# Joining the value and score products of a dilated attention pipeline at the end of an item's 4th and 8th step, with two small moves beside it

## The chip, the cores and the metric

One NeuronCore of a Trainium2 chip runs the whole kernel. Five engines work side by side, each on its own queue of instructions in a fixed order: TensorE (PE, matmuls; its weight loads are shown as PEld), VectorE (DVE), ScalarE (ACT), GpSimd (POOL) and SyncE (SP, which here issues the DMA transfers). They wait for each other by semaphores. SBUF is the working memory of 128 partitions, PSUM the eight banks into which TensorE writes.

The metric is the device time of one execution in microseconds. Before the change it is 1513.78 us, the median of three runs (1512.96 to 1514.76).

## The reference

An encoder block over 1024 positions of 1024 channels, batch 1, in float32. One input projection feeds three mixers; each is gated, projected back, merged with sigmoid gates and passed through an output projection. The part that the change touches is the dilated sliding-window attention: 24 heads of 64 channels, in three groups of eight with the windows and dilations (128, 1), (512, 4) and (2048, 16), whose outputs are merged by the softmax of their log-denominators.

```python
A_GROUPS = ((128, 1), (512, 4), (2048, 16))
...
def dilated_window_attention(q, k, v, window, dilation):
    half = window // (2 * dilation)
    ...
    sc = jnp.einsum('znqhd,znkhd->znhqk', qb, kw).astype(jnp.float32) * (dh ** -0.5)
    sc = jnp.where(valid[None, :, None], sc, NEG_INF)
    m = jnp.max(sc, axis=-1, keepdims=True)
    p = jnp.exp(sc - m)
    l = jnp.sum(p, axis=-1, keepdims=True)
    o = jnp.einsum('znhqk,znkhd->znqhd', (p / l).astype(v.dtype), vw)
    lse = (m + jnp.log(l))[..., 0]
    ...
def reference(x, mem, ...):
    h = rms_norm(x, g_pre[layer])
    a_qkv, bq, bk, bv, mq, ga, gb, gm, mg = jnp.split(h @ w_in[layer], split_at, axis=-1)
    aq = rope(a_qkv[:, :, 0], pos)
    ak = rope(a_qkv[:, :, 1], pos)
    ...
    wts = jax.nn.softmax(jnp.stack(lses, axis=0), axis=0).astype(dt)
    oa = jnp.einsum('gbsh,gbshd->bshd', wts, jnp.stack(outs, axis=0)).reshape(b, s, BRANCH_WIDTH)
    # two more mixers: ob (full attention), om (attention into a memory)
    ya = (oa * jax.nn.silu(ga)) @ w_br_a[layer]
    ...
    merged = gates[:, :, 0] * ya + gates[:, :, 1] * yb + gates[:, :, 2] * ym
    x = x + rms_norm(merged @ w_out[layer], g_post[layer])
```

## The kernel before

Every projection is made of *units* (`add_unit`, L195): 128 output channels over 1024 positions, in two halves of 512. A half is 24 matmuls of `dense` (L139): for each of eight slices of the channels three products (L143, L145, L147) of a rounded high part and a rest of both operands, all into one of two PSUM banks `d`. A unit's weights come by a DMA into one of two buffers `wr` (L114), ScalarE rounds them into `wh` (L105) and VectorE takes the rest into `wl` (L106); this is done one unit ahead.

TensorE's order is written out by hand. `weave` (L174) takes dense matmuls one by one from a generator and puts pieces of attention between them so that both come to their end together: after each piece as many dense matmuls follow as its estimated cost is worth. The order in the other engines' queues is left to a scheduler that follows the program's order and its own estimates.

The dilated attention has twelve *items* (`seq`, L1128): four pairs of heads by three groups. While item n is in work, the three dense units of item n + 1 run: queries, keys, values, 48 matmuls each. Queries and keys are evacuated by `rope_half` (L821): per half, VectorE multiplies the bank by sine and cosine into `t2a` and `t1a` (four products of 32 partitions and one of 128, L830 or L831), and GpSimd adds the two into `aq` or `ak` (L837). For groups 1 and 2 that sum reorders positions into residue classes, so that each half of the positions is spread over the whole tile. The values are evacuated into `vta` (L862).

An item has eight tiles T of 128 queries and these pieces (L1022 to L1030):

- `scores(b)`, for four tiles at a time, into four PSUM banks (L918);
- `soft(T)`: VectorE applies the mask and takes the minimum (L930), ScalarE the exponentials with their sums (L933 to L938), into one of five `pra` buffers;
- `trans(T)`: TensorE transposes the probabilities into the one bank `tr` (L955, L964), ScalarE copies them to `app` (L967);
- `values(i0)`: the values are transposed through the same bank (L895) and copied by ScalarE (L897);
- `pv(b)`: value products for four tiles (L981), copied by ScalarE to `og` (L989);
- `stats`: minima and sums are transposed through the bank `tr` (L1000), copied by VectorE into `sr` (L1003 to L1007) and written out by SyncE.

`plan` (L1032) lists the pieces in steps T = 0 to 7: the soft pass of one tile, the transposes of an earlier one, and at some steps more. An item's second value products (`pv[1]`), its last transposes and its `stats` run in the steps of the next item. When the third group of a pair of heads is done, `combine` (L1079) merges the groups in five steps put at the places of `STEP_T` (L1127): fetch the denominators back, compute the weights, and for each group multiply `og` by a row of weights spread over 64 partitions (L1116). Those rows come through `load` (L1084), two transfers a group into one buffer `wgt`; the next group's transfers can start only when the buffer has been read. GpSimd adds the groups (L1120).

After this stage come the gates, the three branch projections and the output projection.

## Time and profile before

| what | value |
|---|---|
| median of three runs | 1513.78 us |
| profiled execution | 1515.3 us |
| its span, first to last instruction | 1513.5 us |
| busy: TensorE, VectorE, ScalarE, GpSimd | 98%, 56%, 38%, 29% of the span |
| mean granted TensorE clock | 0.997 |
| stage of the dilated attention | about 598 to 1131 us |

In the rows shown below, a row of the timeline reads: start in us from the span's beginning, duration in us, engine, line of the kernel, operation, output<-inputs, shape, and the number of like instructions merged into the row; in brackets the idle time of the engine just before, and what ended it. SPq is SyncE's issuing of transfers. A row of the waits reads: who waited, for whom, total us, times, longest. A row of the windows reads: stretch, its length, then the busy time with the number of instructions of TensorE, of its weight loads, of VectorE, ScalarE and GpSimd, then the granted clock, the DMA engines' share, GB/s. A row of the first part of the page reads: engine, busy us, share of the span, instructions. The duration of a matmul is a modelled latency; matmuls overlap, so the distance from start to start says what one takes.

### The profile page before, as it was taken

The numbers are of one execution on the slowest core, as the hardware profiler recorded it, in microseconds if no ns is written. First come the engines' busy times: TensorE is split into PE (matmuls) and PEld (weight loads), VectorE is DVE, ScalarE is ACT, GpSimd is POOL, SyncE is SP. The second block draws the span as 40 slices with busy tenths as digits, with TensorE's granted clock in tenths as the row PEclk, the third lists the DMA queues.
The fourth block names the chain that finished last, engine by engine and source line by source line (L and its number), as shares of the span: only waits on it lengthen the run. The fifth ranks groups of instructions, "written<-read, shape, count | busy, mean of one in ns | idle before, by whom it ended". The sixth has DMA issues, their size and how long they took to land.

```text
span 1513.5 us, 20622 instructions
## 1 busy us (share of the span) xinstructions
PE 1481.5 (98%) x7844; PEld 1182.4 (78%) x7844; DVE 842.3 (56%) x1526; ACT 574.9 (38%) x1295; POOL 441.3 (29%) x357
## 2 busy tenths in 40 slices
PE   7999989999999999999999999999999999999998
PEld 7899977666776668878777777877777888888787
DVE  7755567566555426655665577466625433525743
ACT  6534444445444431434434444343443112122321
POOL 1426314444444442321232223123200000223322
PEclk9999999999999999999999999999999999999999
DMA  6332011111111122110221122112126531623432
GB/s 239 101 98 71 29 57 51 64 55 42 61 62 57 42 65 83 42 43 29 59 57 57 43 56 59 43 45 71 56 68 207 176 109 42 209 70 112 131 105 98
DMA packets 55043, 119.78 MB, mean 79 GB/s; under 512 B 13792, under 2 KB 23712, under 8 KB 54816
## 3 DMA queue, kind: packets, MB, share of 16 engines
q1 hardware_dynamic: 54800, 118.34, 24.5%
q8 instruction: 61, 1.00, 0.3%
q14 instruction: 38, 0.31, 0.1%
q10 hardware_dynamic: 144, 0.13, 0.0%
HBM read 96.06 MB, written 22.38 MB: 78 GB/s over the span
## 4 chain that ended last, share of the span: by engine, by line
PE 83%; DVE 7%; DMA 3%; issue 3%; ACT 2%; POOL 1%; SPq 0%; DVEq 0%; POOLq 0%; ACTq 0%
PE d L145 14%; PE d L147 13%; PE d L143 13%; PE sc L125 7%; PE ov L720 4%; PE sc L1281 4%; PE sc L147 3%; PE sc L143 3%; PE sc L145 3%; PE ov L981 3%; PE s L918 2%; PE s L705 2%; PE s L704 2%; PE tr L686 2%; PE d L533 2%
## 5 line engine op out<-in xcount | busy, mean ns | idle before, releaser
L147 PE MATMUL d<-hh,wl 128*128 128x512 f32 x992 | 397.8, 401 | 0.0
L145 PE MATMUL d<-hl,wh 128*128 128x512 f32 x992 | 397.6, 401 | 0.0
L143 PE MATMUL d<-hh,wh 128*128 128x512 f32 x992 | 395.0, 398 | 1.7 <-DVE fth L222 1.7
L145 PEld LDWEIGHTS d<-hl,wh 128*128 128x128 f32 x992 | 187.0, 188 | 46.6 <-issue 9.8
L147 PEld LDWEIGHTS d<-hh,wl 128*128 128x128 f32 x992 | 187.2, 189 | 43.3 <-issue 8.0
L143 PEld LDWEIGHTS d<-hh,wh 128*128 128x128 f32 x992 | 187.1, 189 | 42.0 <-issue 3.2
L105 ACT ACTIVATE wh<-wr 128x1024 fp32r<-128x1024 f32 (+1 forms) x100 | 95.3, 954 | 266.8 <-PE sc L145 105.1
L711 POOL TENSOR_TENSOR bl<-bl,bp 128x512 f32<-128x512 f32 x96 | 128.8, 1342 | 141.9 <-ACT bp L707 137.2
L106 DVE TENSOR_TENSOR wl<-wr,wh 128x1024 fp32r<-128x1024 f32 (+1 forms) x100 | 123.4, 1235 | 29.9 <-ACT wh L105 29.7
L687 DVE TENSOR_REDUCE bn<-tr 128x1 f32<-128x512 f32 x128 | 87.6, 689 | 63.5 <-PE tr L686 62.2
L707 ACT ACTIVATE bp<-s 128x512 f32<-128x512 f32 x128 | 75.3, 595 | 84.7 <-PE s L705 84.4
L837 POOL TENSOR_TENSOR aq<-t1a,t2a 128x512 f32<-128x512 f32 x24 | 51.9, 2161 | 187.1 <-DVE t1a L831 187.1
L1182 POOL TENSOR_TENSOR acc<-acc,th 128x1024 f32<-128x1024 f32 x16 | 45.4, 2835 | 202.8 <-DVE th L1181 202.8
L930 DVE CUSTOM_DVE_ANT_0 pra<-s,mask 128x192 f32<-128x192 f32 (+2 forms) x192 | 56.6, 348 | 72.9 <-PE s L918 33.5
L967 ACT ACTIVATE app<-tr 128x384 f32<-128x384 f32 (+2 forms) x96 | 46.0, 480 | 123.7 <-PE tr L964 80.8
L831 DVE SCALAR_TENSOR_TENSOR t2a<-d,tab 32x512 f32<-32x512 f32 x96 | 65.9, 687 | 46.0 <-PE d L147 44.6
L147 PE MATMUL sc<-hh,wl 128*128 128x512 f32 x224 | 87.3, 390 | 1.6 <-DVE wl L106 1.6
L830 DVE TENSOR_TENSOR t2a<-d,tab 32x512 f32<-32x512 f32 x96 | 65.9, 687 | 40.9 <-PE d L147 39.7
L145 PE MATMUL sc<-hl,wh 128*128 128x512 f32 x224 | 87.2, 389 | 0.0
L143 PE MATMUL sc<-hh,wh 128*128 128x512 f32 x224 | 87.1, 389 | 0.0
L837 POOL TENSOR_TENSOR ak<-t1a,t2a 128x512 f32<-128x512 f32 x24 | 54.8, 2284 | 98.5 <-DVE t1a L830 98.5
L938 ACT ACTIVATE pra<-pra,sts 128x128 f32<-128x128 f32 (+2 forms) x152 | 66.6, 440 | 43.6 <-DVE sts L930 43.6
(263 smaller groups left out, 2745.0 us busy)
## 6 DMA issues: line engine op xcount, KB each, us to landing
wr<-in_wu SPq DMA_DIRECT2D x76, 512.0 KB
g2d<-fth SPq DMA_DIRECT2D x24, 256.0 KB
wgt<-wgd SPq DMA_DIRECT2D x24, 256.0 KB
ot<-od SPq DMA_DIRECT2D x12, 512.0 KB
gt<-g2d SPq DMA_DIRECT2D x12, 512.0 KB
wr<-in_wbr SPq DMA_DIRECT2D x24, 256.0 KB
thd<-fth SPq DMA_DIRECT2D x20, 256.0 KB
th<-thd SPq DMA_DIRECT2D x10, 512.0 KB
```

The lines of the kernel that those rows point to most:

```text
L105: A.activation(dst_h, src, AF.Copy)
L106: V.tensor_tensor(dst_l, src, dst_h.bitcast(F32), op=OP.subtract)
L125: PE.matmul(out_ps, a, b, start=i == 0, stop=i == n - 1)
L143: PE.matmul(dst, wh[:, k, :], hh[k][:, t], start=k == 0, stop=False)
L145: PE.matmul(dst, wh[:, k, :], hl[k][:, t], start=False, stop=False)
L147: PE.matmul(dst, wl[:, k, :], hh[k][:, t], start=False, stop=k == 7)
L687: V.tensor_reduce(st[i]["n"][:, j, c:c + 1], s, axis=AX.X, op=OP.min)
L707: A.activation(pp, s, AF.Exp, scale=-1.0)
L711: G.tensor_tensor(lsum[i % 2], lsum[i % 2], pp, op=OP.add)
L830: return V.tensor_tensor(out, x, y, op=OP.mult)
L837: G.tensor_tensor(half_of(o, half, g), classes(t1, g), classes(t2, g), op=OP.add)
L938: A.activation(src, raw, AF.Exp, scale=-1.0, bias=bias, accum_out=sts[:, h, 1, T:T + 1])
```

## The change

In `plan` the value products and the score products are put into one piece by a new helper `joined`: `pv[1]` of the item before with `scores[1]` at the end of step 3, and `pv[0]` with the next item's `scores[0]` at the end of step 7. The steps are renumbered by one, so an item's plan now ends with that joined piece, where it used to go on for another step with the next item's first soft pass and a transpose. Seen from its own pieces an item keeps its order, but for `stats`, which comes directly after the last transposes. `STEP_T` is renumbered with it. The copies of the denominators into `sr` are issued on ScalarE. For the first three pairs of heads the three rows of weights have a buffer each, in the stage's own pool, and are loaded one after the other as soon as they are written; the last pair keeps the one buffer. `t1a` and `t2a` have three buffers instead of two.

```diff
@@ rope_half
-            t1 = aa.tile([P, 512], F32, name="t1a", bufs=2)
-            t2 = aa.tile([P, 512], F32, name="t2a", bufs=2)
+            t1 = aa.tile([P, 512], F32, name="t1a", bufs=3)
+            t2 = aa.tile([P, 512], F32, name="t2a", bufs=3)
@@ stats (the same for g == 0 and g == 1)
-                    V.tensor_copy(sr, tp[0:32, 0, :])
+                    A.activation(sr, tp[0:32, 0, :], AF.Copy)
@@
+        def joined(*pieces):
+            pieces = [x for x in pieces if x]
+            return (lambda: [fn() for fn, _ in pieces]), sum(c for _, c in pieces)
+
         def plan(it, pre, nxt):
...
             if it and not pre:
-                out += [it["scores"][0], it["soft"][0]]
-            for T in range(NT if it else 3):
-                if it and T < 7:
-                    out.append(it["soft"][T + 1])
-                elif nxt and T == 7:
-                    out.append(nxt["soft"][0])
+                out.append(it["scores"][0])
+            for T in range(NT if it else 4):
+                if it:
+                    out.append(it["soft"][T])
                 out.append((lambda T=T: combining(T), 0.0))
-                if T == 0 and pre:
-                    out.append(pre["trans"][7])
-                elif it and T:
-                    out.append(it["trans"][T - 1])
+                if T < 2:
+                    if pre:
+                        out.append(pre["trans"][T + 6])
+                elif it:
+                    out.append(it["trans"][T - 2])
                 if T == 1 and pre:
                     out.append(pre["stats"])
-                if it and 3 <= T < 3 + len(it["values"]):
-                    out.append(it["values"][T - 3])
-                if T == 2:
-                    if pre:
-                        out += [pre["pv"][1], (ready, 0.0)] if it else [pre["pv"][1]]
-                    if it:
-                        out.append(it["scores"][1])
-                if T == 6:
-                    out.append(it["pv"][0])
-                    if nxt:
-                        out.append(nxt["scores"][0])
+                if it and 4 <= T < 4 + len(it["values"]):
+                    out.append(it["values"][T - 4])
+                if T == 3:
+                    out.append(joined(pre and pre["pv"][1], it and it["scores"][1]))
+                    if pre and it:
+                        out.append((ready, 0.0))
+                if T == 7:
+                    out.append(joined(it["pv"][0], nxt and nxt["scores"][0]))
             return out
@@ combine
             def load(g):
-                wgt[g] = cb.tile([P, S], F32, name="wgt", bufs=1)
+                wgt[g] = (aa if p_ < 3 else cb).tile([P, S], F32, name="wgt", bufs=3 if p_ < 3 else 1)
...
-                load(0)
+                for g in range(3 if p_ < 3 else 1):
+                    load(g)
...
-                if g < 2:
+                if g < 2 and p_ == 3:
                     load(g + 1)
@@
-        STEP_T = (3, 5, 7, 1, 4)
+        STEP_T = (4, 6, 0, 2, 5)
```

More of the change, by code (lines that the diff above doesn't have):

```diff
@@ L1002, in stats @@
                 if g == 0:
-                    V.tensor_copy(sr.rearrange("p (b a) -> p b a", b=16), tp[0:32, 0, :].rearrange("p (a b) -> p b a", b=16))
+                    A.activation(sr.rearrange("p (b a) -> p b a", b=16), tp[0:32, 0, :].rearrange("p (a b) -> p b a", b=16), AF.Copy)
                 elif g == 1:
-                    V.tensor_copy(sr.rearrange("p (b a) -> p b a", b=4), tp[0:32, 0, :].rearrange("p (a b) -> p b a", b=4))
+                    A.activation(sr.rearrange("p (b a) -> p b a", b=4), tp[0:32, 0, :].rearrange("p (a b) -> p b a", b=4), AF.Copy)
                 else:
-                    V.tensor_copy(sr, tp[0:32, 0, :])
+                    A.activation(sr, tp[0:32, 0, :], AF.Copy)
                 for h in range(2):
```

## The prediction

> **What bounds the kernel now.** I read the busy shares first, then the stage of the dilated attention (598 to 1131 us) in stretches, then TensorE's own waits there, then the instructions in order of time around three places.

> ```profile
> PE 1481.5 (98%) x7844; PEld 1182.4 (78%) x7844; DVE 842.3 (56%) x1526; ACT 574.9 (38%) x1295; POOL 441.3 (29%) x357
> ```

> ```profile
> 598.00:1131.00 533.00, 527.16 (x3154) 418.74 (x3155) 312.58 (x733) 221.00 (x660) 131.31 (x79) 1.00 0.17 51
> 772.00:818.00 46.00, 43.92 (x274) 34.63 (x274) 29.91 (x63) 18.12 (x56) 17.27 (x10) 1.00 0.24 70
> ```

> ```profile
> PE tr L955 <- DVE sr L1003: 4.6, 3, 1.7
> ```

> TensorE is the bound. In the 533 us that the change touches it is idle for 533.00 - 527.16 = 5.8 us, and 2.1 us of that lies in the one stretch shown. So an edit gains only by taking matmul time away or by ending one of those idle spots; and anything that makes TensorE wait costs its full length.

> The idle spot of that stretch:

> ```profile
> 775.77 2.05 DVE L1116 TENSOR_TENSOR og<-og,wgt 128x1024 f32<-128x1024 f32 x1 [1.30 <-DMA wgt<-wgd]
> 778.72 2.75 DVE L106 TENSOR_TENSOR wl<-wr,wh 128x1024 fp32r<-128x1024 f32 x1
> 781.39 0.27 DVE L1003 COPY sr<-tr 32x128 f32<-32x128 f32 x1
> ```

> ```profile
> 779.63 0.39 PE L143 MATMUL d<-hh,wh 128*128 128x512 f32 x1
> 781.72 0.55 PE L955 MATMUL tr<-cs,pra 128*128 128x128 f32 x3 [1.70 <-DVE sr L1003]
> ```

> ```profile
> 782.36 0.49 ACT L967 ACTIVATE app<-tr 128x384 f32<-128x384 f32 x1 [3.84 <-PE tr L955]
> ```

> VectorE waits for a weight row's DMA, does the weighting and a split, and only then copies the denominators out of the single transpose bank; TensorE waits for that bank. ScalarE stands idle for 3.84 us there.

> **The change, part by part.**

> *Denominators copied by ScalarE, and one step earlier.* ScalarE is free where the copy falls, so the three waits go: -4.6 us, with the row above as the most that can go and 0 as the least. The other nine copies held nobody up and still don't: in the changed program five dense matmuls (four for group 2) stand between the denominators' transpose and the next user of the bank.

> *All weights loaded together.* The same 24 transfers; for the first three head pairs six go out at once.

> ```profile
> 771.37 4.31 DMA wgt<-wgd
> ```

> ```profile
> 748.22 1.13 SPq L1087 DMA_DIRECT2D wgt<-wgd  x2
> 753.09 11.53 SPq L114 DMA_DIRECT2D wr<-in_wu  x2
> ```

> ```profile
> 775.48 1.05 ACT L105 ACTIVATE wh<-wr 128x1024 fp32r<-128x1024 f32 x1
> ```

> Two transfers took 4.31 us, so six take about 13 us and end near 761. The weights of a dense unit issued behind them at 753.09 are split at 775.48 (two buffers: they refill the one just freed and are used the time after next), some 10 us after they would land even if they ran last. Hidden: 0. If that cover went, the split and then a unit would be late. The 1.30 us that VectorE waits for the second row goes, but VectorE is not the bound. The weighting of group 1 now stands ahead of the value evacuation (L862) in VectorE's queue: from the score products on, VectorE has about 1 us of latency, six mask passes of 0.28 us and two weightings of 2 us, 6.7 us, and the evacuation then takes 1.1. TensorE wants that bank again 34 dense matmuls and the scores themselves later, some 9.5 us on: 0, with 1.7 us to spare.

> *Three buffers for t1a and t2a* (L824, L825): no wait of VectorE for GpSimd stands in the list at L830 or L831, so 0.

> *Value and score products joined.* In the issue order of the two programs the dilated stage has 189 stretches of dense matmuls before and 167 after: 22 joins. What a stretch costs at its edges:

> ```profile
> 758.17 0.60 PE L964 MATMUL tr<-cs,pra 128*128 128x128 f32 x4
> 758.53 0.48 PE L143 MATMUL d<-hh,wh 128*128 128x512 f32 x1
> 758.84 0.39 PE L145 MATMUL d<-hl,wh 128*128 128x512 f32 x1
> 759.07 0.40 PE L147 MATMUL d<-hh,wl 128*128 128x512 f32 x1
> 759.54 0.40 PE L145 MATMUL d<-hl,wh 128*128 128x512 f32 x1
> 759.86 1.97 PE L981 MATMUL ov<-app,avs 128*64 128x128 f32 x32
> 761.76 0.50 PE L147 MATMUL d<-hh,wl 128*128 128x512 f32 x1
> 762.10 0.39 PE L143 MATMUL d<-hh,wh 128*128 128x512 f32 x1
> 766.43 0.39 PE L145 MATMUL d<-hl,wh 128*128 128x512 f32 x1
> 766.75 1.56 PE L918 MATMUL s<-ak,aq 64*128 64x192 f32 x15
> ```

> ```profile
> 849.34 0.39 PE L147 MATMUL d<-hh,wl 128*128 128x512 f32 x1
> 850.81 1.09 PE L981 MATMUL ov<-app,avs 128*64 128x128 f32 x16
> 851.84 0.50 PE L145 MATMUL d<-hl,wh 128*128 128x512 f32 x1
> 855.01 1.89 PE L918 MATMUL s<-ak,aq 64*128 64x192 f32 x16
> ```

> Dense matmuls start 0.23 us apart (758.84 to 759.07). The step into a product piece is 0.32 (759.54 to 759.86, 766.43 to 766.75), and the first dense step after one is 0.34 (761.76 to 762.10): 0.09 and 0.11 too much. Inside, 32 value matmuls take 1.90 and 16 take 1.03, so 0.109 a pair and 0.16 over for both ends together. Leaving one piece and entering the next thus costs about 0.40: 0.11 + 0.10 out, 0.09 + 0.10 in. The join takes that away and puts in one edge from value to score products, which this trace doesn't show. Its bounds are 0 and 0.40; I take 0.20, the price of one edge, since shapes still change (128x64 to 64x128). 22 x 0.20 = -4.4 us, between -8.8 and 0. [...]

> *Where the joined pieces now fall.* This is the part that costs. An item's last piece is now value products followed at once by the next item's first score products, and its pieces end one step later against the dense units. The scores need the keys, whose rotary product comes from the second of the three units. In issue order, the dense matmuls between the end of that unit and the scores are:
> - group 1: 23 before (24 in the first), 9 after (10);
> - group 2: 28 before, 14 after;
> - group 0: 17 before, 10 after.

> How long the keys take after their last dense matmul:

> ```profile
> 759.58 2.79 DVE L830 TENSOR_TENSOR t2a<-d,tab 32x512 f32<-32x512 f32 x4 [2.94 <-PE d L147]
> 763.01 1.22 DVE L106 TENSOR_TENSOR wl<-wr,wh 128x1024 fp32r<-128x1024 f32 x1
> ```

> ```profile
> 756.72 2.14 POOL L837 TENSOR_TENSOR ak<-t1a,t2a 128x512 f32<-128x512 f32 x1 [4.74 <-DVE t1a L830]
> 763.17 3.07 POOL L837 TENSOR_TENSOR ak<-t1a,t2a 128x512 f32<-128x512 f32 x1 [4.31 <-DVE t1a L830]
> 810.48 2.99 POOL L837 TENSOR_TENSOR ak<-t1a,t2a 128x512 f32<-128x512 f32 x1 [4.58 <-DVE t1a L830]
> 853.43 2.19 POOL L837 TENSOR_TENSOR ak<-t1a,t2a 128x512 f32<-128x512 f32 x1 [5.14 <-DVE t1a L830]
> ```

> ```profile
> 806.39 0.40 PE L147 MATMUL d<-hh,wl 128*128 128x512 f32 x1
> 815.55 1.16 PE L918 MATMUL s<-ak,aq 64*128 64x128 f32 x16
> ```

> From the last dense matmul to the end of GpSimd's sum: group 1: 763.17 + 3.07 - 759.07 = 7.17 us; group 2: 810.48 + 2.99 - 806.39 = 7.08; group 0: 853.43 + 2.19 - 849.34 = 6.28. Before, the scores start after 766.75 - 759.07 = 7.68, 815.55 - 806.39 = 9.16 and 855.01 - 849.34 = 5.67 us (group 0's first three score tiles need only the first half of the keys; the fourth, some 1.3 us on, needs the second). So the old order leaves 0.5 us for group 1.

> The new arrival is the old one, less the dense matmuls taken out, less one edge pair with half of it put back (0.20), plus the transposes that now stand there instead of earlier (four of them 0.36 + 0.31 - 0.23 = 0.44, fewer in proportion):
> - group 1: 7.68 - 14 x 0.231 - 0.20 + 0.44 + 0.11 = 4.80; keys at 7.17 + 0.06 (781.72 less the copy's end at 781.66): waits 2.4 us. The first item has one dense matmul more: 2.2.
> - group 2: 9.16 - 14 x 0.231 - 0.20 + 0.44 = 6.17; 7.14: waits 1.0.
> - group 0: 5.67 - 7 x 0.231 - 0.20 + 0.22 = 4.07, the fourth tile at 5.37; 6.34: waits 1.0.

> Four items of group 1, four of group 2, three of group 0: 2.2 + 3 x 2.4 + 4 x 1.0 + 3 x 1.0 = 16.4 us. Nothing covers it: the queue is in order, and behind the waiting scores stand the dense matmuls and everything else. Below nothing it can't be. Its bounds: 6 us if each sum took 0.93 us less (as the first half's does, 2.14 against 3.07), and 22 us if VectorE came to the keys 0.5 us later each time.

> The second join of an item (its 4th step) needs score banks that VectorE has read: the last of those passes ends some 5 us after an item's dense units begin, and the scores come 31 dense matmuls, four pieces and the value products later, over 10 us. It waits for nothing.

> *The tail* (the last head pair keeps one weight buffer; the order of its DMAs is unchanged): 0.

> **Sum**, against the profiled execution's 1515.3 us (span 1513.5): -4.6 - 4.4 + 16.4 = +7.4, 1522.7. That execution lies 1.5 above the median of the three runs, 1513.8, so the forecast is **1521 us**.

> **The rivals.**

> 1. *The scores don't wait, or hardly* (faster): the two gains stand alone, 1513.8 - 9.0 = 1504.8 us. For it speaks that the old scores of group 0 do begin before GpSimd's sum has ended. Against it: for groups 1 and 2 both halves of the keys interleave, and the scores can't start on half of them. It decides as soon as the eleven waits sum to under 9 us, 0.8 each, that is if the keys come 0.7 us sooner than they do today. Chance 0.08.

> 2. *GpSimd's sum gets ahead of the split's subtraction.* The subtraction (763.01, L106) begins 0.16 us before the sum (763.17), and the sum then takes 3.07 instead of 2.14. If the rounding on ScalarE (L105) comes a little later in the new order, the sum runs first and each wait shrinks by 0.93: 2.2 + 3 x 2.4 + 7 x 1.0 less that is 6.2 us, and the time 1513.8 - 9.0 + 6.2 = 1511 us. Against it: the rounding waits for the same dense unit to end as before. Chance 0.07. [...]

> 3. *VectorE is late too.* The weightings now come two in a row ahead of the value evacuation, and passes of the mask stand between the two halves of the keys. Each further 1 us at the keys' second half costs 11 us: 1532. It begins when VectorE is still busy as that half ends; in the trace it stood idle for 2.94 us there (the row at 759.58). Chance 0.13.

> 4. *No change that can be told.* Half the waits I count with the gains as counted: 1513.8 - 9.0 + 8.2 = 1513. Chance 0.10.

> **How the numbers follow.** The forecast itself (waits of 12 to 20 us, joins worth 2 to 7) holds 1517 to 1527 and 0.62. What a measurement of this kernel can tell from no change is about 0.2%, 3 us: 1510.8 to 1516.8. Rivals 2 and 4 lie within that, most of them: same 0.15. Rival 1 and a little of 2 are faster: 0.10. The forecast and rival 3 are slower: 0.75. The range reaches from rival 2's value to near rival 3's: 1510 to 1530 leaves out rival 1 and half of rival 3.

> **What would show it.** Right: in the list of TensorE's waits a new row, the score products (now still L918) waiting for GpSimd's sum of keys (L837), 11 or so times, longest about 2.4 us, some 16 us in all; the row of the transposes waiting for the denominators' copy gone; value products followed by scores with about 0.2 us of edge between; TensorE idle some 18 us between 598 and 1140 instead of 5.8; VectorE never waiting for the weights in the first three pairs. Wrong: scores that follow the value products without an idle note (rival 1); a sum of 2.1 us for the second half (rival 2); products waiting for the masks, or dense matmuls for VectorE's evacuation (rival 3); a value-to-score edge of 0.4 or more, which would take the join's gain away; or a new wait of TensorE for ScalarE's copy.

## The result and the profile after

The changed kernel takes 1524.17 us, median of six runs (1518.37 to 1525.66), against 1514.27 for the kernel before (1512.73 to 1515.14, the three runs shown above and three beside the changed kernel). The ratio is 1.0062, with a 95% interval of 1.0045 to 1.0079: slower. The profiled execution took 1525.66 us, its span is 1523.8, its mean granted clock 0.992 (before: 0.997).

The busy shares after, first part of the page:

```profile
PE 1485.2 (97%) x7844; PEld 1189.5 (78%) x7844; DVE 833.6 (55%) x1514; ACT 580.0 (38%) x1307; POOL 443.0 (29%) x357
```

TensorE has the same 7844 matmuls and is yet 3.7 us longer busy. Twelve instructions (the denominators' copies) have gone from VectorE to ScalarE.

TensorE's waits in the dilated stage after (line, what it waited for: us in total, times, longest):

```profile
PE s L918 <- POOL ak L837: 10.9, 11, 2.0
PE tr L895 <- ACT app L967: 1.5, 5, 0.3
PE tr L1000 <- ACT app L967: 1.1, 3, 0.5
PE tr L964 <- ACT app L967: 0.3, 1, 0.3
```

The wait for the denominators' copy is gone. In its place the scores wait eleven times for GpSimd's sum of the keys, and the transposes a little longer for ScalarE's copy out of the transpose bank: 2.9 us in the last three rows, where the kernel before had 1.2.

One join of group 1, TensorE's and GpSimd's instructions in order of time (start, duration, [wait and what released it]):

```profile
626.31 0.39 PE L147 MATMUL d<-hh,wl 128*128 128x512 f32 x1
629.21 0.40 PE L143 MATMUL d<-hh,wh 128*128 128x512 f32 x1
629.54 1.97 PE L981 MATMUL ov<-app,avs 128*64 128x128 f32 x32
633.47 2.56 PE L918 MATMUL s<-ak,aq 64*128 64x192 f32 x16 [1.97 <-POOL ak L837]
635.96 0.79 PE L145 MATMUL d<-hl,wh 128*128 128x512 f32 x1
```

```profile
630.40 3.02 POOL L837 TENSOR_TENSOR ak<-t1a,t2a 128x512 f32<-128x512 f32 x1 [5.02 <-DVE t1a L830]
```

The last matmul of the keys starts at 626.31; the sum ends at 633.42 and the scores start at 633.47. That much was forecast. What follows was not: the scores take 2.56 us where the kernel before had 1.56, and the dense matmul behind them 0.79 instead of 0.50. The same profile cut into stretches shows why (stretch; its length, then busy time of PE, PEld, DVE, ACT, POOL; granted clock, DMA share, GB/s):

```profile
598.00:1140.00 542.00, 527.91 (x3137) 423.32 (x3137) 304.48 (x721) 225.12 (x671) 133.30 (x79) 0.99 0.17 51
633.90:637.30 3.40, 3.40 (x18) 2.77 (x16) 1.84 (x12) 2.07 (x11) 0.00 (x0) 0.50 0.10 41
770.40:773.80 3.40, 3.40 (x17) 2.67 (x15) 2.87 (x8) 1.70 (x8) 0.00 (x0) 0.50 0.09 33
907.00:910.40 3.40, 3.40 (x17) 2.77 (x16) 2.53 (x7) 1.70 (x8) 0.00 (x0) 0.50 0.09 36
1043.50:1046.90 3.40, 3.40 (x19) 2.77 (x16) 2.36 (x7) 1.71 (x8) 0.00 (x0) 0.50 0.12 47
```

Four stretches of 3.4 us have a granted clock of 0.50: one behind each of the four waits of group 1, the long ones. By that clock each does in 3.4 us what full clock does in 1.7. Between the first two, from 637.5 to 763, the clock is 1.00.

The difference of the two profiled spans, 1523.8 - 1513.5 = 10.3 us, thus comes out as: idle time 542.00 - 527.91 = 14.1 instead of 5.8, that is +8.3; four half-clock stretches, 4 x 1.7 = +6.8; the joins' edges, -4.4 (below). The sum is +10.7. It comes this near partly by chance: outside this stage TensorE is 1.6 us less idle than before (0.4 ahead of it, 1.2 behind it), and with that the sum is 9.1, so 1.2 us stay unassigned.

### The profile page after: what moved, and what is told of

Read it like the earlier page. It is cut to its first block, busy times and chain, and to the rows that moved or that the text cites. A ratio compares the mean times of both kernels' runs of the same rounds, so it can differ in the third digit from the quotient of the medians.

```text
span 1523.8 us, 20621 instructions
## 1 busy us (share of the span) xinstructions
PE 1485.2 (97%) x7844; PEld 1189.5 (78%) x7844; DVE 833.6 (55%) x1514; ACT 580.0 (38%) x1307; POOL 443.0 (29%) x357
## 5 line engine op out<-in xcount | busy, mean ns | idle before, releaser
L143 PE MATMUL d<-hh,wh 128*128 128x512 f32 x992 | 397.3, 400 | 1.7 <-DVE fth L222 1.7
L145 PE MATMUL d<-hl,wh 128*128 128x512 f32 x992 | 397.6, 401 | 0.0
L147 PE MATMUL d<-hh,wl 128*128 128x512 f32 x992 | 394.4, 398 | 0.0
L143 PEld LDWEIGHTS d<-hh,wh 128*128 128x128 f32 x992 | 187.8, 189 | 44.9 <-issue 5.5
L145 PEld LDWEIGHTS d<-hl,wh 128*128 128x128 f32 x992 | 187.9, 189 | 44.4 <-issue 8.7
L105 ACT ACTIVATE wh<-wr 128x1024 fp32r<-128x1024 f32 (+1 forms) x100 | 95.5, 956 | 330.6 <-PE sc L145 105.3
L147 PEld LDWEIGHTS d<-hh,wl 128*128 128x128 f32 x992 | 187.6, 189 | 40.9 <-issue 4.2
L106 DVE TENSOR_TENSOR wl<-wr,wh 128x1024 fp32r<-128x1024 f32 (+1 forms) x100 | 113.8, 1139 | 28.3 <-ACT wh L105 28.1
L837 POOL TENSOR_TENSOR aq<-t1a,t2a 128x512 f32<-128x512 f32 x24 | 54.8, 2283 | 195.7 <-DVE t1a L831 168.0
L831 DVE SCALAR_TENSOR_TENSOR t2a<-d,tab 32x512 f32<-32x512 f32 x96 | 65.9, 687 | 59.6 <-PE d L147 58.5
L967 ACT ACTIVATE app<-tr 128x384 f32<-128x384 f32 (+2 forms) x96 | 46.0, 479 | 120.9 <-PE tr L964 72.5
L830 DVE TENSOR_TENSOR t2a<-d,tab 32x512 f32<-32x512 f32 x96 | 65.9, 687 | 42.4 <-PE d L147 31.7
L147 PE MATMUL sc<-hh,wl 128*128 128x512 f32 x224 | 87.2, 390 | 1.1 <-DVE wl L106 1.1
L145 PE MATMUL sc<-hl,wh 128*128 128x512 f32 x224 | 87.1, 389 | 0.0
L143 PE MATMUL sc<-hh,wh 128*128 128x512 f32 x224 | 87.1, 389 | 0.0
L837 POOL TENSOR_TENSOR ak<-t1a,t2a 128x512 f32<-128x512 f32 x24 | 54.2, 2260 | 97.4 <-DVE t1a L830 97.4
L125 PE MATMUL sc<-gh,wh 128*128 128x512 f32 x192 | 74.7, 389 | 0.0
```

Of the source, the lines that this page charges most:

```text
L105: A.activation(dst_h, src, AF.Copy)
L106: V.tensor_tensor(dst_l, src, dst_h.bitcast(F32), op=OP.subtract)
L125: PE.matmul(out_ps, a, b, start=i == 0, stop=i == n - 1)
L143: PE.matmul(dst, wh[:, k, :], hh[k][:, t], start=k == 0, stop=False)
L145: PE.matmul(dst, wh[:, k, :], hl[k][:, t], start=False, stop=False)
L147: PE.matmul(dst, wl[:, k, :], hh[k][:, t], start=False, stop=k == 7)
```

## The experiments

**Denominators alone.** The kernel before with one edit (the same in all three branches):

```diff
-                    V.tensor_copy(sr, tp[0:32, 0, :])
+                    A.activation(sr, tp[0:32, 0, :], AF.Copy)
```

> The kernel before with one edit: the denominators are copied by ScalarE. If VectorE's lateness with that copy is what holds TensorE at the transposes, the three waits of 4.6 us go and the time falls to about 1514.3 - 4.6 = 1509.7 us, with no row of transposes waiting for that copy. If another wait takes its place (ScalarE late, or the next reader of the bank), the time stays within 1 us of 1514.3.

Measured: 1510.55 us against 1514.71, ratio 0.9974 (0.9964 to 0.9984), so 4.1 us less. What is left of TensorE's waits in this stage:

```profile
PE tr L895 <- ACT app L967: 1.2, 3, 0.4
```

The part is worth what was forecast. So the rest of the change costs 9.9 + 4.1 = 14 us.

**The join of the 8th step taken apart.** The changed kernel with

```diff
-                    out.append(joined(it["pv"][0], nxt and nxt["scores"][0]))
+                    out += [it["pv"][0]] + ([nxt["scores"][0]] if nxt else [])
```

> The changed kernel with the join at the 8th step undone: the value products and the next item's scores are two pieces again there, so 21 dense matmuls stand between them and the scores begin about 5 us later; the join at the 4th step stays. If the scores' wait for the keys, and the half clock that follows it, are what made the change slower, both go and the time is 1514.3 - 4.6 (copy) - 11 joins x 0.2 = about 1507.5 us with a granted clock of 0.997. If the loss came from something else in the change (the step's shift, ScalarE's copy, the loads), it stays at 1518 or more.

Measured: 1520.39 us, ratio 1.0039 (1.0027 to 1.005): 13 us above what was expected, and within what was expected if the loss came from something else in the change. The time alone thus doesn't settle it. The scores no longer wait, but TensorE does elsewhere. Its costliest wait in this stage, one instance of it, and ScalarE and VectorE around that instance:

```profile
PE tr L1000 <- ACT app L967: 8.2, 6, 2.4
```

```profile
781.96 0.28 PE L1000 MATMUL tr<-cs,sts 128*32 128x128 f32 x1 [2.34 <-ACT app L967]
```

```profile
780.27 0.46 ACT L938 ACTIVATE pra<-pra,sts 128x192 f32<-128x192 f32 x1 [2.90 <-DVE sts L930]
781.44 0.47 ACT L967 ACTIVATE app<-tr 128x384 f32<-128x384 f32 x1
```

```profile
771.49 2.02 DVE L1117 TENSOR_TENSOR og<-og,wgt 128x1024 f32<-128x1024 f32 x1
774.26 2.04 DVE L1117 TENSOR_TENSOR og<-og,wgt 128x1024 f32<-128x1024 f32 x1
...
777.22 2.74 DVE L106 TENSOR_TENSOR wl<-wr,wh 128x1024 fp32r<-128x1024 f32 x1
779.88 0.34 DVE L930 CUSTOM_DVE_ANT_0 pra<-s,mask 128x192 f32<-128x192 f32 x1
```

To be read from VectorE upwards: it does two weightings, the value evacuation (left out here) and a split before a mask pass. The split takes 2.74 us instead of the 1.22 that it takes in a row further down (775.23): it began while GpSimd's sum of two groups (L1121) was at work, 776.47 to 778.87, while in that other row it began before the sum (775.49 there). The profile of the kernel before has the same two cases in this stage: six splits that begin while such a sum is at work take 2.75 to 2.83 us, as the one at 778.72 (the sum runs from 777.99 to 780.38), and all others 1.22 to 1.27. Then ScalarE, whose queue is in order, stands 2.90 us in an exponential that needs that mask pass; behind the exponential stands the copy out of the single transpose bank (781.44 to 781.91), and the denominators' transpose starts at 781.96. This wait, too, is followed by half clock, in three places. 1507.5 expected + 8.2 + 3 x 1.7 = 1520.8, as measured.

**The keys sooner.** The changed kernel with the sum of the keys' second half on VectorE:

```diff
-            G.tensor_tensor(half_of(o, half, g), classes(t1, g), classes(t2, g), op=OP.add)
+            (E or G).tensor_tensor(half_of(o, half, g), classes(t1, g), classes(t2, g), op=OP.add)
...
-                    rope_half(d[name], half, p, scale, g)
+                    rope_half(d[name], half, p, scale, g, V if name == "k" and half else G)
```

> The changed kernel with one edit: the rotary sum of the keys' second half is made by VectorE, right behind its products, and not by GpSimd; the order of TensorE is untouched. The keys should be ready about 5 us after their last dense matmul and not 7.1, which is at or before the scores' arrival in groups 1 and 2 (4.8 and 6.8 us) and in time for the fourth tile of group 0. If GpSimd's sum is what the scores wait for: waits under 3 us in all instead of about 12, no stretch at half clock in this stage, 1505 to 1508 us. If the wait is for something else (the banks, the queries), the time stays at 1521 to 1525.

Measured: 1512.55 us, ratio 0.9984 (0.9975 to 0.9994).

```profile
PE s L918 <- DVE ak L837: 4.9, 7, 1.1
```

The wait was for GpSimd's sum, then, but the forecast of 1505 to 1508 us is missed by some 5. Waits of at most 1.1 us are left, 4.9 in all where under 3 were expected: in front of the sum VectorE does the split (630.27, 1.22 us), so the sum runs from 631.40 to 632.46 and the keys come 6.15 us after their last matmul (626.31), not 5. There is no half clock: the clock is 0.996 to 0.997 in its runs. Against the changed kernel the waits for the keys shrink by 6.0 us, the time by 11.6. Idle time alone doesn't account for that; the rest, 5.6, is near the price of the four half-clock stretches.

**The wait filled with work.** The changed kernel with seven dense matmuls of no use into a score bank that the scores then overwrite, ahead of each item's first scores of group 1:

```diff
+                        if g == 1 and b == 0 and j == 0:
+                            for _ in range(7):
+                                PE.matmul(banks[0], hh[0][:, 0:128], hh[0][:, 0:512], start=True, stop=True)
```

> The changed kernel with work added: ahead of the first scores of each item of group 1, in the place where TensorE stood idle for about 2 us, seven useless 128x512 matmuls are put into a score bank that the scores then overwrite. If the half clock comes because TensorE is idle in that place, the four stretches at half clock go, and the kernel with more work is faster: about 1524 - 6.7 = 1517 to 1518 us, granted clock 0.997 in all runs. If the half clock has nothing to do with the wait, the time is 1523 to 1526 us and the stretches are still there.

Measured: 1519.17 us, ratio 1.0031 (1.002 to 1.0042), a little above the 1517 to 1518 expected. Its waits and its whole stage (columns as above; the three added lines shift L918 to L921):

```profile
PE s L921 <- POOL ak L837: 3.7, 11, 0.8
```

```profile
598.00:1140.00 542.00, 535.06 (x3199) 428.47 (x3196) 306.23 (x729) 226.82 (x674) 133.44 (x79) 1.00 0.17 51
```

More work, the scores no earlier, and 5.0 us less than the changed kernel. The clock is 0.997 in all runs but one (0.995). Here the half clock goes with TensorE's idle time: the value and score products are all still there, and with waits of at most 0.8 us they didn't bring it.

**The pieces held back.** The changed kernel with the pieces of attention paced 8% behind the dense units, so that the pair at the 8th step comes later:

```diff
-            weave(len(FILL_A) if last else 3, run(pieces), sum(c for _, c in pieces), 1.0)
+            weave(len(FILL_A) if last else 3, run(pieces), sum(c for _, c in pieces), 1.0 if last else 0.92)
```

> The changed kernel with one number changed: in all items but the last the attention pieces are spread at 0.92 of the pace, so that the joined piece at the 8th step falls about nine dense matmuls (2.1 us) later against the keys' unit. Nothing is taken apart. If the change lost its time because the scores come before the keys: waits for the keys of about 2 us in all at most, no stretch at half clock in this stage, both joins' gain kept: 1514.7 - 4.1 (copy) - 4.4 (joins) + 2 = about 1508 us. If the joins themselves cost time, 1515 or more.

Measured: 1510.98 us, ratio 0.9979 (0.9964 to 0.9994), 3 us above what was expected.

```profile
PE tr L1000 <- ACT app L967: 7.9, 4, 2.8
```

The scores' wait is gone with the joins kept; the wait for ScalarE's copy comes up in its place, as when the join was taken apart, with two half-clock stretches in the profile.

**`stats` back at its old step**, for both of these:

```diff
-                if T == 1 and pre:
+                if T == 2 and pre:
                     out.append(pre["stats"])
```

With the 8th-step join apart:

> The run with the join at the 4th step alone, and the denominators' transpose put back one step later, to its place before. In that run TensorE waited 8.2 us at this transpose for ScalarE's copy of the transposes before it, with three stretches at half clock. If the earlier place of this transpose is what holds it, both go and the time is 1514.7 - 4.1 - 11 x 0.2 = about 1508.5 us. If the joined piece at the 4th step delays ScalarE wherever that transpose stands, the wait moves with it and the time stays near 1520.

With the pieces held back:

> Both mends together: pace 0.92 in all items but the last, and the denominators' transpose in its place before. All that the change gains and nothing that it loses: 1514.7 - 4.1 (copy) - 4.4 (22 joins) = about 1506 us, some 4 us under the kernel before with ScalarE's copy alone (1510.6), which would price the joins. If the joins are worth nothing, 1510 to 1511.

Measured: 1512.68 (ratio 0.9988, 0.9979 to 0.9997) and 1508.59 us (0.9962, 0.9951 to 0.9974). The waits of the one, then of the other:

```profile
PE tr L955 <- ACT app L967: 4.3, 3, 1.5
```

```profile
PE tr L955 <- ACT app L967: 5.5, 3, 1.9
```

Part of the wait went, part moved on to the next transposes (L955). `stats` was only the first in the queue to meet it. The expectations were 4.2 and 2.6 us too good. The second of these kernels has two half-clock stretches in its profile, the first none.

**The old loads in it.** The last kernel, with the weights loaded one group at a time through one buffer and two buffers for `t1a` and `t2a` again:

```diff
-                wgt[g] = (aa if p_ < 3 else cb).tile([P, S], F32, name="wgt", bufs=3 if p_ < 3 else 1)
+                wgt[g] = cb.tile([P, S], F32, name="wgt", bufs=1)
...
-                for g in range(3 if p_ < 3 else 1):
-                    load(g)
+                load(0)
...
-                if g < 2 and p_ == 3:
+                if g < 2:
```

> The kernel with both mends, with the weights loaded one after the other through one buffer as before and two buffers for t1a and t2a. I priced loading together and the third buffers at nothing: the same time as with both mends, within 1 us. If VectorE's waits for the weights reach TensorE (through the masks and evacuations behind them), it is 2 to 5 us slower.

Measured: **1504.82 us** (1504.55 to 1505.19), ratio 0.9935 (0.992 to 0.995). This is faster than both kernels, and 3.8 us faster than with all weights loaded together, where no difference was expected. The edit takes back the loads and the third buffers at once; that the loads are what counts is read from the order below and not tried alone. TensorE's wait for ScalarE's copy, 5.5 us above:

```profile
PE tr L955 <- ACT app L967: 1.4, 3, 0.6
```

VectorE's order at one place, first with all weights loaded together, then with the old loads:

```profile
770.89 2.04 DVE L1117 TENSOR_TENSOR og<-og,wgt 128x1024 f32<-128x1024 f32 x1 [4.00 <-DMA wgt<-wgd]
773.30 2.02 DVE L1117 TENSOR_TENSOR og<-og,wgt 128x1024 f32<-128x1024 f32 x1 [0.37 <-DMA wgt<-wgd]
775.23 1.22 DVE L106 TENSOR_TENSOR wl<-wr,wh 128x1024 fp32r<-128x1024 f32 x1
776.37 0.35 DVE L930 CUSTOM_DVE_ANT_0 pra<-s,mask 128x192 f32<-128x192 f32 x1
```

```profile
771.39 2.05 DVE L1116 TENSOR_TENSOR og<-og,wgt 128x1024 f32<-128x1024 f32 x1 [3.88 <-DMA wgt<-wgd]
...
774.31 1.25 DVE L106 TENSOR_TENSOR wl<-wr,wh 128x1024 fp32r<-128x1024 f32 x1
775.44 0.38 DVE L930 CUSTOM_DVE_ANT_0 pra<-s,mask 128x192 f32<-128x192 f32 x1
778.16 2.02 DVE L1116 TENSOR_TENSOR og<-og,wgt 128x1024 f32<-128x1024 f32 x1 [2.06 <-DMA wgt<-wgd]
```

With the old loads the second weighting's row comes later (VectorE waits 2.06 us for it), and the mask pass stands ahead of that weighting instead of behind it: it starts 0.93 us sooner (775.44 against 776.37).

**The old loads in the changed kernel itself**, the same edit there:

> The changed kernel with the weights loaded one after the other through one buffer, and two buffers for t1a and t2a, as before; joins, steps and ScalarE's copy as changed. With both mends this edit was worth 3.8 us, because VectorE's queue no longer had two weightings ahead of the masks that ScalarE waits for. In the changed kernel 53 dense matmuls stand between the scores and the denominators' transpose, against 45 and 32 in the runs where it waited, so that delay should be covered: 1523 to 1525 us, as the changed kernel. If loading together costs as much there, about 1520.

Measured: 1525.34 us against 1515.08, ratio 1.0077 (1.006 to 1.0095). The intervals of this ratio and the changed kernel's overlap: no price of loading together can be told there. The reason given in the expectation, that the delay is covered, doesn't hold, for the old loads make TensorE wait more at the denominators' transpose, where the changed kernel has 1.1 us:

```profile
PE tr L1000 <- ACT app L967: 5.0, 6, 1.4
```

Against these 3.9 us its profile has only one half-clock stretch instead of four, 5.1 us less, and the two spans differ by 1.4. So what loading together costs depends on what else is late.

**Both joins taken apart in the fastest version:**

```diff
-                    out.append(joined(pre and pre["pv"][1], it and it["scores"][1]))
+                    out += [x for x in (pre and pre["pv"][1], it and it["scores"][1]) if x]
...
-                    out.append(joined(it["pv"][0], nxt and nxt["scores"][0]))
+                    out += [it["pv"][0]] + ([nxt["scores"][0]] if nxt else [])
```

> The fastest run so far (both mends, weights loaded as before) with both joins taken apart and nothing else changed: its value and score products are pieces of their own again, with dense matmuls between. A joined piece took 0.20 us less than its two halves apart, in every shape, so 22 x 0.20 = 4.4 us come back: 1504.8 + 4.4 = about 1509 us. If the joins gain or lose elsewhere as well, through the time that the scores come, it is off from that by more than 1.5 us.

Measured: 1529.89 us, ratio 1.01 (1.0085 to 1.0116), 21 us off. The products' edges are as expected. First joined, in the fastest version, then the same two pieces apart:

```profile
761.02 0.40 PE L147 MATMUL d<-hh,wl 128*128 128x512 f32 x1
761.35 1.97 PE L981 MATMUL ov<-app,avs 128*64 128x128 f32 x32
763.25 1.57 PE L918 MATMUL s<-ak,aq 64*128 64x192 f32 x16
764.75 0.50 PE L143 MATMUL d<-hh,wh 128*128 128x512 f32 x1
765.09 0.40 PE L145 MATMUL d<-hl,wh 128*128 128x512 f32 x1
```

```profile
762.87 0.40 PE L147 MATMUL d<-hh,wl 128*128 128x512 f32 x1
763.19 1.97 PE L981 MATMUL ov<-app,avs 128*64 128x128 f32 x32
765.43 0.39 PE L145 MATMUL d<-hl,wh 128*128 128x512 f32 x1
...
770.22 0.39 PE L145 MATMUL d<-hl,wh 128*128 128x512 f32 x1
770.53 1.57 PE L918 MATMUL s<-ak,aq 64*128 64x192 f32 x16
772.38 0.40 PE L143 MATMUL d<-hh,wh 128*128 128x512 f32 x1
```

Joined, 761.02 to 765.09 less two dense steps of 0.23 is 3.61 us; apart, 2.56 and 2.16 less two steps each is 2.10 + 1.70 = 3.80. A join saves 0.19. The rest of the 25 us is waiting:

```profile
PE tr L955 <- ACT avs L897: 8.9, 3, 3.0
PE tr L955 <- ACT app L967: 5.6, 3, 2.0
```

At this pace and without joins the scores of groups 1 and 2 at an item's end come 23 dense matmuls later and leave 11 and 6 of them, instead of 34 and 29, before the next transposes, whose copy out of the bank stands on ScalarE behind exponentials of those scores. At 0.23 us each that is 5 us less for VectorE and ScalarE, and three half-clock stretches come on top. The two waits, less the 1.4 us of the fastest version, make 13.1, the stretches 3 x 1.7 = 5.1 and the edges 4.4: together 22.6 of the 25 us. In this kernel a join is worth more for when it brings the scores than for its edges.

## Why the prediction was right, and where it was not

The direction held, and 1524 lies 3 us above the forecast of 1521, within its range. The terms agree less well than the sum:

| step | forecast, us | measured, us |
|---|---|---|
| denominators' copies | -4.6 | -4.1 (in the kernel before) |
| loads together, three buffers | 0 | no difference that can be told |
| 22 joins | -4.4 | 0.19 to 0.20 each (in the fastest version), -4.2 to -4.4 |
| scores wait for keys | +16.4 | +10.9 |
| half clock behind the waits | not in it | +6.8 in the profiled execution |
| transposes' other waits | not in it | +1.7 |

Against the median of the runs before: 1514.3 - 4.1 - 4.4 + 10.9 + 6.8 + 1.7 = 1525.2; the profiled execution took 1525.7, the median is 1524.2.

- **The scores' wait** was the right mechanism, at all eleven places, and the size was 5.5 us too large in all. Group 1 was forecast at 2.2 and 2.4 an item, and its rows show 1.95 to 1.97: 1.6 us of the 5.5. Group 0 was forecast at 1.0 and shows 0.76 and 0.77, at the fourth tile as forecast: 0.7 us. The largest part, 3.2 us, is group 2, forecast at 1.0 and measured at 0.20:

```profile
674.45 0.47 PE L147 MATMUL d<-hh,wl 128*128 128x512 f32 x1
675.94 0.66 PE L895 MATMUL tr<-cs,vda 128*128 128x128 f32 x4 [0.32 <-ACT app L967]
679.40 1.97 PE L981 MATMUL ov<-app,avs 128*64 128x128 f32 x32
681.57 1.16 PE L918 MATMUL s<-ak,aq 64*128 64x128 f32 x16 [0.20 <-POOL ak L837]
```

  The keys are ready at 681.57 - 674.45 = 7.1 us, as forecast (7.14), but without waiting the scores would have arrived at 679.40 + 1.90 - 674.45 = 6.85 instead of 6.17. For 0.32 us of that the value transposes in between wait for ScalarE, and a wait in front takes off a wait behind; the other 0.36 lies in the edges of the pieces and isn't separated here.
- **"Nothing covers it"** was true, but I priced the wait at its own length only, with the clock at full speed behind it. This is the step that failed: the terms of the sum lacked the half clock. That the sum still came near is luck in part: this omission (6.8) and that of the transposes' waits (1.7) stand against the 5.5 us by which the scores' wait was too large, and the 3.0 left over are about the 3 us above the forecast. Without the half clock the measured terms give 1514.3 - 4.1 - 4.4 + 10.9 + 1.7 = 1518.4, and the one run of the changed kernel at clock 0.997 took 1518.37.
- **The joins:** the edge from value to score products costs 0.20, the middle of the bounds: a join saved 0.19 to 0.20 of the 0.40 that it would have saved with a free edge.
- **Loads at 0** came out right here, but not for the reason given. I looked at the value evacuation as what stands behind the second weighting in VectorE's queue. Behind it stand also the mask passes, and behind those ScalarE's exponentials, its copy and TensorE's bank. In the kernel with `stats` in place and the pieces held back this costs 3.8 us. In the changed kernel it is loading one at a time that lets TensorE wait 3.9 us more there, with fewer half-clock stretches against it.
- **The rivals:** the scores do wait (not 1); the sum of the second half takes 3.02 us at 630.40 and the split's subtraction still comes first (not 2); VectorE was not late at the keys in the changed kernel, it stood idle for 3.64 us before their second half at 626.81 (not 3), though the cause that this rival named, long weightings ahead of short passes, is what met the repaired versions. No change (4) is excluded by the interval. Of the signs named, VectorE indeed never waits for the weights in the first three pairs, and TensorE is idle for 14.1 us, not 18. One sign of being wrong did come, though small: three new waits for ScalarE's copy at the denominators' transpose, 1.1 us.

## What to carry to other kernels

When pieces are joined to save an edge, work out when each of them must now start and what it waits for: here the 0.20 us that a join saves were outweighed several times over by the waits of an in-order queue, while the same joins with the pieces held back 8% and the old loads and `stats` place kept make a kernel that takes 0.9935 of the time before. A wait of the bounding engine near 2 us can cost almost twice its length, 2.0 + 1.7 us here. Loading earlier is not free either (3.8 us in the version with the pieces held back and `stats` in place), if it lets a scheduler put a long instruction ahead of a short one that other engines need.

## What was not expected of the hardware

Where the stretches begin accounts for this. Cut finely, the trace of the changed kernel has them begin at 633.89, 770.43, 906.96 and 1043.49, each 136.53 us after the one before. The first ends at 637.31, so that a stretch lasts 3.41 us, and 136.53 is 40 x 3.413; the half clock ahead of this stage begins at 210.64, 124 x 3.413 before the first, and lasts two such lengths, to 217.47. Other profiles show the same grid, each from a start of its own, to within a few hundredths of a us: with the pieces held back stretches begin at 780.52 and 913.64 (39 lengths apart), with `stats` back as well at 779.20 and 912.32 (39), and in the fastest version without joins at 917.36, 944.68 and 1084.60 (8 and 41). In the interval of the grid just before a stretch TensorE was idle for 1.85 to 2.65 us, 15 times (1.95 to 1.97 in the changed kernel); the other intervals of this stage, in all twelve profiles, have at most 1.88. The changed kernel with the old loads shows both cases, with four waits of 1.96 or 1.97 us. These are the intervals that hold most of the first wait and of the second:

```profile
631.98:635.39 3.41, 1.44 (x18) 1.28 (x16) 0.44 (x4) 0.60 (x1) 1.99 (x1) 1.00 0.48 154
768.51:771.92 3.41, 1.55 (x17) 1.33 (x17) 0.60 (x5) 0.68 (x2) 1.80 (x1) 1.00 0.49 159
```

The first wait lies whole in its interval, 3.41 - 1.44 = 1.97 us idle, and half clock follows. The ends of the intervals cut the other three, so that 1.86, 1.77 and 1.45 us lie in one, and none follows. In these profiles it is the idle time within one interval that counts, with the bound near 1.9 us, and not the length of the wait.
